# New planning constants (four waits of a recurrence chain, two matmul prices) in a decoder layer on one core

## The chip, the core and the metric

The kernel runs on one core of one Trainium2 chip. The metric is the device time of one execution in microseconds (us), the median over several runs. PE is the matrix engine, DVE the vector engine, ACT the scalar engine, POOL the GpSimd engine; SP only issues DMAs. Each engine takes its instructions in the order in which they stand in its own queue, and semaphores make one engine wait for another.

## What is computed

One decoder layer on 2048 tokens of 1024 channels, in float32. A projection of the normed input feeds two branches; one of them is a delta-rule recurrence over the tokens, with 8 heads of a 64x64 state. Their gated sum is projected and added, then come a squared-ReLU MLP, an embedding gate and a last norm. In short:

```python
h = rmsnorm(x, g_mix);  z = h @ w_in
# branch A, for each token and head:
sa = einsum('bhvk,bhk->bhv', S, -kk)
S  = S * w + sa * (kk * a) + v * k
y  = einsum('bhvk,bhk->bhv', S, r)
y_a = (groupnorm(y) + bonus) * g @ w_out_a
# branch B: causal means over 2, 4, 8 and 16 tokens, a map per group, @ w_out_b
x = x + (sigmoid(gA) * y_a + sigmoid(gB) * y_b) @ w_o
x = x + relu(rmsnorm(x) @ w_ff1)**2 @ w_ff2
x = x + sigmoid(rmsnorm(x) @ w_ple_gate) * (p @ w_ple_proj)
return rmsnorm(x, g_final)
```

## The kernel before

**Dense work.** A float32 product is made as three products of split parts (hi and lo in a reduced format), each a 128x512 matmul with a `d` tile of PSUM as its output (`mm3`, `mm`, L133). Stage A (four blocks of 512 tokens) makes the projection, the pooling branch and the gates; stage B (four blocks) makes the two output projections and the residual. The MLP and the embedding gate come after both, from about 1660 us on, with no recurrence beside them.

**The recurrence** runs over 32 chunks of 64 tokens, called iterations here, all heads at once. One iteration is cut into pieces, each written as a generator that yields how long its next piece has to wait:

- `prep`: builds the chunk's matrices. On PE: `rkr`/`rd` sums, `bdb` and `bdk` products, `bdv` and `BK` transposes.
- `invert`: a triangular inverse, on DVE. Its input goes through memory (`aD`, loaded as `At`), and after one step at L859 to L863 it runs 16 pairs of L869 (product into `Xtmp`) and L872 (sum into `Xt`). The first pair is 128x16 wide in the trace, the second 128x32, and so on to 128x256; in the order lists the same widths read 128x8x2, 128x8x4, and so on to 128x8x32. The result goes through memory (`xD`) into `xd`.
- `chain`: the serial part, from state `SV` to the next state. Its five PE steps are: TL (`rc<-SV,TL`), the first `xd` product (`rc<-Tn,xd`), `aof` (`rc<-U,aof`), the second `xd` product (`rc<-Tn,xd` again), and `NB` (`rc<-VU,NB`), with the outputs (`RD`, `Ct`) right behind it. Between the steps ACT or DVE moves a result: L887 and L904 on ACT, **L911** (a DVE subtraction into `Tn`, between `aof` and the second `xd` product), and L918 and L920 (DVE and ACT copies into `VU`, between the second `xd` product and `NB`).
- `gnorm`: the group norm of the chunk, one PE step (`ybd` transposes).

**What sets the order.** PE's order is written out by `drive`, a planner that runs when the program is built. It keeps a planned clock, `clock[0]`. Every matmul that is emitted adds its price to it (in `mm`, and 0.109 for a transpose). A recurrence piece is emitted once the planned clock has passed the time it yielded (an entry of `LAT`); until then `drive` emits dense matmuls, mostly three at a time. The entries used in `chain` are `hop` (TL to first `xd`), `hu` (first `xd` to `aof`, and, before the change, `aof` to second `xd` too), `hv` (second `xd` to `NB`) and `hs` (the end of the chain). Other entries time the prep (`A`, `B1`, `C0`, `C1`, `C`), the inverse (`inv`: `bdb` to the first `xd` product), the norm (`gn`) and the least distance between iterations (`pace`, and `pace2` for the last quarter). None of these waits is in the program itself: the real waits are semaphores, and PE stands still when it reaches a step whose operand isn't there.

The order on DVE, ACT, POOL and SP is not written by hand. A scheduler of the framework makes it when the program is built, from priorities (recurrence pieces are emitted at high priority) and from the PE order it is given. So a new PE order also changes the order on the others.

Of the kernel before, what the change touches and what calls it, by code (L numbers as in the profile page):

```python
# [10 lines left out]
F32 = mybir.dt.float32  # L11
# [29 lines left out]
WS, WS2, WS3, WSB = 384, 384, 512, 512  # L41

LAT = dict(p0=11.7, p0b=15.8, A=17.7, B0=2.1, B1=5.6, C0=2.0, C1=4.9, C=8.8,
           hop=3.1, hu=2.8, hv=5.3, hs=3.0, inv=47.1, gn=17.8, pace=34.4, pace2=31.5)
TC_KW = dict(schedule_with_timeline_sim=True)

W1 = NP * UT
# [51 lines left out]
def hybrid_kernel(ctx, tc, consts, x, p, g_mix, w_in, mu_shift, w0, w_decay_up, a0, w_aaa_up,  # L99
# [26 lines left out]
    clock = [0.0]  # L126

    def mm(out_, lhsT, rhs, start, stop, **kw):
        n = 1
        for d in rhs.shape[1:]:  # L130
            n *= d
        clock[0] += max(0.107, n * (4 if rhs.dtype == F32 else 1) / 2370.0)
        PE.matmul(out_, lhsT, rhs, start=start, stop=stop, **kw)  # L133

    def tr(out_, in_, idn):
# [51 lines left out]
    def mm3(ps, st, mv, first, last):  # L187

        mm(ps, st[0], mv[0], first, False)
        mm(ps, st[0], mv[1], False, False)  # L190
        mm(ps, st[1], mv[0], False, last)
# [4 lines left out]
    with ExitStack() as c1:  # L196
# [443 lines left out]
        def cps():  # L640
            return psum.tile([P, 512], F32, name="rc", tag="rc", bufs=2)
# [5 lines left out]
        def v3(t, w=UT):  # L647
            return t.rearrange("p (n t) -> p n t", t=w)

        def pq(t):  # L650

            return t.rearrange("p (q t) -> p q t", t=L)

        def wt(name, bufs=1, w=W1):
            return rw.tile([P, w], F32, name=name, bufs=bufs)
# [219 lines left out]
        def chain(i):  # L875

            c_ = carried[i]
            dl, xd, aof, Ct, NB, TL, RD, SV, VU = (c_[n] for n in ("dl", "xd", "aof", "Ct", "NB", "TL", "RD", "SV", "VU"))
            SVn = bd["SV"][(i + 1) % 2]
            Y = rw.tile([P, PC, L], F32, name="Y", bufs=2)  # L880
            c_["Y"] = Y
            qs = [(q, slice(q * L, (q + 1) * L), slice(q * P, (q + 1) * P)) for q in range(PC)]

            def diag(out_, ps):

                for hp in hps:
                    ACT.copy(out=out_(hp), in_=v3(ps, P)[hp, :, hp])  # L887
            ps = cps()
            for q, sl, wl in qs:
                mm(ps[:, wl], TL[:, q, :], SV[:, q, :], True, True)  # L890
            Tn = wt("Tn")
            diag(lambda hp: pq(Tn)[hp], ps)
            yield HOP
            q2s = [slice(a * P, (a + 1) * P) for a in range(PC // 2)]

            def quarters(src, inv):

                for n, (lo, b) in enumerate((h * L + b * SUB, b) for h in range(2) for b in range(2)):
                    yield n, VU[lo:lo + SUB, b ^ inv::2, lo // L * L:(lo // L + 1) * L], pq(src)[lo:lo + SUB, b ^ inv::2, :]
            ps = cps()  # L900
            for a, sl in enumerate(q2s):
                mm(ps[:, sl], xd[:, 2 * a, :], Tn[:, sl], True, True)
            Ua = wt("U")
            ACT.copy(out=Ua, in_=ps[:, 0:W1])  # L904
            for _, to, fr in quarters(ps[:, 0:W1], 0):
                ACT.copy(out=to, in_=fr)
            yield LAT["hu"]
            ps = cps()
            for a, sl in enumerate(q2s):
                mm(ps[:, sl], aof[:, a, :], Ua[:, sl], True, True)  # L910
            DVE.tensor_tensor(Tn, Tn, ps[:, 0:W1], ALU.subtract)  # L911
            yield LAT["hu"]
            ps = cps()
            for a, sl in enumerate(q2s):
                mm(ps[:, sl], xd[:, 2 * a + 1, :], Tn[:, sl], True, True)
            for n, to, fr in quarters(ps[:, 0:W1], 1):
                if n % 2:
                    DVE.tensor_copy(to, fr)  # L918
                else:
                    ACT.copy(out=to, in_=fr)  # L920
            yield LAT["hv"]
            ps = cps()
            for q, sl, wl in qs:
                mm(ps[:, wl], NB[:, q, :], VU[:, q, :], True, True)
            for hp in hps:
                DVE.tensor_tensor(SVn[hp, :, hp], v3(ps, P)[hp, :, hp], SV[hp, :, hp], ALU.add)
            for hp in hps:
                DVE.tensor_tensor(SVn[hp, :, hp], SVn[hp, :, hp], dl[hp].unsqueeze(2).broadcast_to([L, PC, L]), ALU.mult)
            py = cps()
            for q, sl, wl in qs:  # L930
                mm(py[:, wl], RD[:, q, :], SV[:, q, :], True, False)
                mm(py[:, wl], Ct[:, q, :], VU[:, q, :], False, True)
            diag(lambda hp: Y[hp], py)
            yield LAT["hs"]
# [48 lines left out]
        def admit():  # L983
            kinds = [k for k, *_ in active]
            i = counts["p0"]
            if i < NU and i == counts["a"] and i not in p0 and z_done[i // NG * UT // TB]:
                with tc.high_priority():
                    p0[i] = prep0(i)
                p0_ready[i] = clock[0] + (LAT["p0b"] if i % (NG * TB // UT) == 0 else LAT["p0"])
                counts["p0"] += 1  # L990
            i = counts["a"]
            if i in p0 and passed[0] >= i - 1 and max(p0_ready[i], passed[1]) <= clock[0]:
                with tc.high_priority():
                    pa[i] = prep_a(i)
                began[0] = clock[0]
                pa_ready[i] = clock[0] + LAT["A"]
                counts["a"] += 1
            i = counts["prep"]
            if "prep" not in kinds and i in pa and i < counts["gn_done"] + 3:
                active.append(["prep", i, prep(i), pa_ready[i], None])  # L1000
                counts["prep"] += 1
            i = counts["chain"]
            if "chain" not in kinds and i < counts["prep_done"] and i < counts["gn_done"] + 2:
                active.append(["chain", i, chain(i), chain_ready[i], None])
                counts["chain"] += 1
# [353 lines left out]
```

## Time and profile before

| | |
|---|---|
| median of 3 runs (lowest to highest) | 3357.87 us (3354.74 to 3360.87) |
| the profiled execution | 3362.13 us, span 3360.3 us |
| PE busy over the span | 3196.8 us (95%) |
| DVE, ACT, POOL busy | 60%, 35%, 28% |
| 0 to 1650 us (recurrence beside dense work): PE idle | some 150 us |
| 1650 to 3360 us (MLP and after): PE idle | 11.6 us |

The profile counts an engine as busy while an instruction of it runs. Matmuls overlap, so their single durations are longer than the distance from one to the next. The granted clock is the share of TensorE's full speed that the hardware let through. A row of the timeline has start, duration, engine, line, operation, output<-inputs and a count; brackets hold the idle time just before it, and what the trace holds to have ended it. Float32 matmuls of the recurrence are recorded as two instructions each (x4 in the trace for two products).

### The profile page before, as it was taken

How to read it: one execution, taken by the hardware profiler on the slowest of the kernel's cores; microseconds unless marked ns; L12 is line 12 of the kernel's file. 1: busy time of each engine (PE TensorE's matmuls, PEld its weight loads, DVE VectorE, ACT ScalarE, POOL GpSimd, SP SyncE). 2: the span in 40 equal slices, each digit the busy share in tenths (PEclk: the TensorE clock that was granted, in tenths of full speed). 3: DMA queues.
4: the chain of work that ended last, by engine and by line, in shares of the span. 5: the costliest groups of instructions: out<-in, count | busy, mean ns of one | idle time of the engine just before them, and what ended most of it. 6: DMA issues, size and time to landing. Idle time of an engine off the chain costs nothing.

```text
span 3360.3 us, 43232 instructions
## 1 busy us (share of the span) xinstructions
PE 3196.8 (95%) x15177; PEld 2620.5 (78%) x15177; DVE 2021.1 (60%) x5020; ACT 1182.4 (35%) x2406; POOL 950.1 (28%) x1162
## 2 busy tenths in 40 slices
PE   7989999999999997889899999999999999999998
PEld 6777777777878786668688888888788888888887
DVE  4489888788887879873643333333775333333375
ACT  4445544554455444431322222211332222221132
POOL 4655444344434435421111111111102111111110
PEclk9999999999999998999999999999999999999999
DMA  8866767666766567778741111110233111111021
GB/s 249 243 216 205 245 205 236 222 212 186 227 218 219 175 209 235 234 242 290 275 140 51 51 51 51 44 51 26 83 131 113 51 51 51 51 47 47 26 65 60
DMA packets 391030, 485.60 MB, mean 145 GB/s; under 512 B 168158, under 2 KB 298268, under 8 KB 367644
## 3 DMA queue, kind: packets, MB, share of 16 engines
q1 hardware_dynamic: 390812, 482.83, 45.1%
q8 instruction: 120, 1.97, 0.2%
q14 instruction: 98, 0.80, 0.1%
HBM read 363.21 MB, written 119.54 MB: 144 GB/s over the span
## 4 chain that ended last, share of the span: by engine, by line
PE 70%; DVE 14%; DMA 7%; ACT 3%; issue 3%; POOL 2%; SPq 1%; DVEq 0%; POOLq 0%; ACTq 0%
PE d L133 63%; DVE Xtmp L869 3%; PE rc L133 3%; PE rp L133 3%; DMA At<-aD 2%; DVE Xt L872 1%; ACT sq L961 1%; DMA aD<-Ast 1%; DMA wf<-wc 1%; DMA t2k<-yaD 1%; PE rp L137 1%; DVE wf L238 1%; DVE Apr L859 1%; PE rc L137 1%; SPq L789 0%
## 5 line engine op out<-in xcount | busy, mean ns | idle before, releaser
L133 PE MATMUL d<-big,wf 128*128 128x512 f32 (+1 forms) x3288 | 840.6, 403 | 17.6 <-DVE wf L238 9.2
L133 PEld LDWEIGHTS d<-big,wf 128*128 128x128 f32 x3288 | 608.9, 192 | 150.2 <-DVE wf L238 11.7
L133 PE MATMUL d<-wf,rt 128*128 128x512 f32 x3072 | 722.4, 395 | 0.0
L133 PE MATMUL d<-hT,wf 128*128 128x512 f32 x3072 | 700.1, 389 | 0.6 <-DVE hT L185 0.4
L133 PEld LDWEIGHTS d<-wf,rt 128*128 128x128 f32 x3072 | 574.9, 187 | 139.7
L133 PEld LDWEIGHTS d<-hT,wf 128*128 128x128 f32 x3072 | 576.5, 188 | 121.6 <-DVE hT L185 0.7
L1099 POOL TENSOR_TENSOR wf<-wr,wf 128x512 fp32r<-128x512 f32 x146 | 256.8, 1764 | 1396.1 <-ACT wf L1095 1394.5
L1215 DVE TENSOR_TENSOR xa<-xa,d 128x512 f32<-128x512 f32 x256 | 175.7, 686 | 410.0 <-PE d L133 409.6
L1095 ACT CAST wf<-wr 128x1024 fp32r<-128x1024 f32 x148 | 153.4, 1045 | 688.7 <-PE d L133 570.0
L1159 DVE TENSOR_TENSOR t<-t,d 128x512 f32<-128x512 f32 x128 | 87.9, 687 | 274.9 <-ACT t L1158 274.9
L869 DVE TENSOR_TENSOR Xtmp<-Xt,At 128x16 f32<-128x16 f32 (+15 forms) x512 | 238.3, 465 | 9.3
L133 PE MATMUL d<-yx,wf 128*128 128x512 f32 x768 | 210.0, 420 | 25.7 <-ACT yx L387 15.8
L133 PE MATMUL d<-wf,big 128*128 128x512 f32 x768 | 190.5, 401 | 11.0 <-DVE t2k L608 9.2
L1158 ACT ACTIVATE t<-d 128x512 f32<-128x512 f32 x128 | 76.6, 599 | 347.3 <-PE d L133 347.3
L133 PEld LDWEIGHTS d<-yx,wf 128*128 128x128 f32 x768 | 150.1, 202 | 62.1 <-ACT yx L387 17.5
L1099 DVE TENSOR_TENSOR wf<-wr,wf 128x512 fp32r<-128x512 f32 (+1 forms) x148 | 115.8, 783 | 131.3 <-ACT wf L1095 130.9
L133 PE MATMUL d<-wf,hT 128*128 128x512 f32 x768 | 183.6, 394 | 0.0
L1161 DVE TENSOR_TENSOR rt<-t,rt 128x512 fp32r<-128x512 f32 x128 | 154.0, 1203 | 45.3 <-ACT rt L1160 45.3
L133 PEld LDWEIGHTS d<-wf,big 128*128 128x128 f32 x768 | 143.0, 191 | 43.7 <-DVE t2k L608 11.1
L133 PEld LDWEIGHTS d<-wf,hT 128*128 128x128 f32 x768 | 143.9, 188 | 33.6
L872 DVE TENSOR_REDUCE Xt<-Xtmp 128x8 f32<-128x16 f32 (+15 forms) x512 | 147.5, 288 | 9.4
L238 POOL TENSOR_TENSOR wf<-wr,wf 128x640 fp32r<-128x640 f32 (+2 forms) x69 | 121.1, 1756 | 76.4 <-ACT wf L235 71.8
(225 smaller groups left out, 3921.3 us busy)
## 6 DMA issues: line engine op xcount, KB each, us to landing
wf<-wc SPq DMA_DIRECT2D x131, 1024.0 KB, 5.7
wr<-in_w_ff_dram SPq DMA_DIRECT2D x128, 512.0 KB, 4.0
wc<-wf SPq DMA_DIRECT2D x50, 1024.0 KB, 6.3
wr<-in_w_in_dram SPq DMA_DIRECT2D x51, 512.0 KB, 4.4
zD<-t2k SPq DMA_DIRECT2D x96, 256.0 KB, 4.7
zs<-zD SPq DMA_DIRECT2D x32, 640.0 KB, 6.4
At<-aD SPq DMA_DIRECT2D x32, 512.0 KB, 4.8
xt<-in_x_dram SPq DMA_DIRECT2D x28, 512.0 KB, 6.9
```

Source lines behind the costliest of these rows:

```text
L133: PE.matmul(out_, lhsT, rhs, start=start, stop=stop, **kw)
L137: PE.transpose(out_, in_, idn)
L238: eng.tensor_tensor(wf[:, 1, c], raw[:, c], hi.bitcast(F32)[:, c], ALU.subtract)
L859: DVE.tensor_tensor(pr, Ab[:, :, :, e:e + 1].broadcast_to([P, SUB, nb, lvl]), dgv[:, :, o:o + lvl].unsqueeze(1).broadcast_to([P, SUB, nb, ...
L869: DVE.tensor_tensor(tmp[:, :, :, 0:n], Xt[:, :, 0:n].unsqueeze(2).broadcast_to([P, MCOL, FS, n]), At[:, 0:n, r:n].rearrange("p s r -> p r ...
L872: DVE.tensor_reduce(Xt[:, :, r:n].unsqueeze(3), tmp[:, :, :, 0:n], AX.X, ALU.add)
L1095: ACT.copy(out=hi, in_=raw[:, 0:k * n])
L1099: eng.tensor_tensor(wf[:, 1, c], raw[:, c], hi.bitcast(F32)[:, c], ALU.subtract)
L1158: ACT.activation(out=t, in_=ps, func=AF.Relu)
L1159: DVE.tensor_tensor(t, t, ps, ALU.mult)
L1161: DVE.tensor_tensor(rt[:, 1, cs], t, rt[:, 0, cs].bitcast(F32), ALU.subtract)
L1215: DVE.tensor_tensor(xa[j][:, ns], xa[j][:, ns], ps, ALU.add)
```

## The change

Four planned waits of the chain get other values: `hop` 3.1 to 2.5, `hv` 5.3 to 5.8, `hs` 3.0 to 4.2, and the wait between `aof` and the second `xd` product, which was `hu` (2.8), gets an entry of its own, `ht` = 6.2. The prices in `mm` change too: a 128x512 matmul of split parts goes from 0.216 to 0.2265, a float32 one of 128x128 from 0.216 to 0.22, and one of 64 columns from 0.108 to 0.22. All other entries of `LAT` stay. No instruction is added or taken away.

```diff
@@ -41,7 +41,7 @@
 LAT = dict(p0=11.7, p0b=15.8, A=17.7, B0=2.1, B1=5.6, C0=2.0, C1=4.9, C=8.8,
-           hop=3.1, hu=2.8, hv=5.3, hs=3.0, inv=47.1, gn=17.8, pace=34.4, pace2=31.5)
+           hop=2.5, hu=2.8, ht=6.2, hv=5.8, hs=4.2, inv=47.1, gn=17.8, pace=34.4, pace2=31.5)
@@ -129,7 +129,7 @@
-        clock[0] += max(0.107, n * (4 if rhs.dtype == F32 else 1) / 2370.0)
+        clock[0] += max(0.22, n / 595.0) if rhs.dtype == F32 else max(0.11, n / 2260.0)
         PE.matmul(out_, lhsT, rhs, start=start, stop=stop, **kw)
@@ -909,7 +909,7 @@
             DVE.tensor_tensor(Tn, Tn, ps[:, 0:W1], ALU.subtract)
-            yield LAT["hu"]
+            yield LAT["ht"]
```

What this does to PE's order is seen in the fifth iteration, from its `aof` step to its `NB` step. Here `big,wf` and `yx,lrw` are dense matmuls; all else is recurrence. Before:

```order
L133 MATMUL rc<-U,aof_242 128x128 x2
L133 MATMUL d<-big,wf 128x512 x15
L133 MATMUL rc<-Tn,xd_236 128x128 x2
L133 MATMUL d<-big,wf 128x512 x6
L133 MATMUL d<-yx,lrw 128x512 x3
L133 MATMUL d<-big,wf 128x512 x9
L133 MATMUL rp<-rkr,bor 128x256 x2
L133 MATMUL rp<-rd,hbr 128x256
L133 MATMUL d<-big,wf 128x512 x6
L133 MATMUL rc<-VU_254,NB 128x128 x4
```

The same stretch of the same iteration in the changed program:

```order
L133 MATMUL rc<-U,aof_242 128x128 x2
L133 MATMUL d<-big,wf 128x512 x15
L137 MATMUL rp<-ident,ybd_240 128x128 x4
L133 MATMUL d<-big,wf 128x512 x6
L133 MATMUL rp<-rkr,bor 128x256 x2
L133 MATMUL rp<-rd,hbr 128x256
L133 MATMUL d<-yx,lrw 128x512 x3
L133 MATMUL rc<-Tn,xd_236 128x128 x2
L133 MATMUL d<-big,wf 128x512 x21
L133 MATMUL rp<-AR,bdb_226 128x128 x4
L133 MATMUL d<-big,wf 128x512 x3
L133 MATMUL rc<-VU_254,NB 128x128 x4
```

Between `aof` and the second `xd` product there were 15 dense matmuls; now there are 24, the `ybd` transposes (which stood ahead of `aof` before) and the `rkr`/`rd` sums (which stood behind the `xd` product). Between that product and `NB` there are 24 dense matmuls in both, and the next iteration's `bdb` in place of the sums. Counted over the first 23 iterations, from one TL to the next, there were 2832 dense matmuls and are now 2746.

On DVE the scheduler puts L911 at another place. This is its queue in the same iteration, up to L911; the L869/L872 pairs belong to the inverse of the following iteration. Before:

```order
L869 TENSOR_TENSOR Xtmp<-Xt,At 128x8x18
L872 TENSOR_REDUCE Xt<-Xtmp 128x4x2
L869 TENSOR_TENSOR Xtmp<-Xt,At 128x8x20
L872 TENSOR_REDUCE Xt<-Xtmp 128x4x2
L238 TENSOR_TENSOR wf<-wr,wf 128x384
L869 TENSOR_TENSOR Xtmp<-Xt,At 128x8x22
L872 TENSOR_REDUCE Xt<-Xtmp 128x4x2
L911 TENSOR_TENSOR Tn<-Tn,rc 128x256
```

DVE's queue up to the same L911 in the changed program:

```order
L869 TENSOR_TENSOR Xtmp<-Xt,At 128x8x14
L872 TENSOR_REDUCE Xt<-Xtmp 128x4x2
L869 TENSOR_TENSOR Xtmp<-Xt,At 128x8x16
L458 SCALAR_TENSOR_TENSOR t2k<-ze,vec,t2k 128x512
L872 TENSOR_REDUCE Xt<-Xtmp 128x4x2
L911 TENSOR_TENSOR Tn<-Tn,rc 128x256
```

L911 stood behind the 11th of the 16 pairs and now stands behind the 8th. Over the first 24 iterations it stood behind 12.3 pairs on average and now stands behind 7.7.

## The prediction

> **What bounds the kernel now.** The page comes first: which engine is full, and where not.
>
> ```profile
> PE 3196.8 (95%) x15177; PEld 2620.5 (78%) x15177; DVE 2021.1 (60%) x5020; ACT 1182.4 (35%) x2406; POOL 950.1 (28%) x1162
> PE   7989999999999997889899999999999999999998
> DVE  4489888788887879873643333333775333333375
> ```
>
> PE is the bound. Its idle time lies in the first 20 slices (to 1680 us), where DVE is at 80% too; the change touches only the recurrence there. So the end moves by what PE loses in that part and by nothing else: the same matmuls are issued in either order. The view by stages, cut at the TL steps of the first iteration and of the 24th and at the last chain, sizes the loss.
>
> ```profile
> core 0: us, PE busy (x) PEld busy (x) DVE busy (x) ACT busy (x) POOL busy (x), PEclk, DMA share, GB/s
> 216.20:1176.40 960.20, 896.77 (x4751) 742.96 (x4750) 817.49 (x2395) 504.30 (x1181) 419.31 (x671) 0.97 0.68 213
> 1176.40:1527.40 351.00, 301.28 (x1550) 247.89 (x1549) 285.59 (x781) 142.94 (x342) 131.97 (x174) 0.94 0.70 231
> ```
>
> In 23 iterations PE is idle 63.4 us, and the granted clock of 0.97 costs about 29 more (0.03 x 960). An iteration takes 41.7 us (960.2/23) and needs 35.5 us of DVE (817.5/23). The groups of PE's instructions, from 216 to 1216 us, say at which step it stands idle (last column: idle time before the group).
>
> ```profile
> L133 PE MATMUL rc<-Tn,xd 128*128 128x128 f32 x192 | 33.5, 301 | 42.2 <-issue 32.9 <-ACT zp L509 4.9 <-ACT t2k L488 2.6
> L133 PE MATMUL d<-big,wf 128*128 128x512 f32 x2452 | 641.8, 407 | 13.1 <-ACT wf L235 5.6 <-DVE wf L238 4.7 <-DMA wf<-wc 2.5
> L133 PE MATMUL rc<-U,aof 128*128 128x128 f32 x96 | 15.6, 288 | 6.1 <-ACT U L904 6.1
> L133 PE MATMUL rc<-VU,NB 128*128 128x128 f32 x192 | 25.4, 275 | 1.7 <-DVE VU L918 1.7
> L133 PE MATMUL rc<-SV,TL 128*128 128x128 f32 x193 | 25.5, 274 | 0.0
> ```
>
> 42.2 us of it stands at the `xd` products. The names of releasers there mislead; the timeline of the fifth iteration on PE and on DVE shows who is late.
>
> ```profile
> 395.29 0.60 PE L137 MATMUL rp<-ident,ybd 128*128 128x128 f32 x4
> 395.72 0.61 PE L133 MATMUL rc<-U,aof 128*128 128x128 f32 x4
> 396.09 3.68 PE L133 MATMUL d<-big,wf 128*128 128x512 f32 x15
> 403.28 1.19 PE L133 MATMUL rc<-Tn,xd 128*128 128x128 f32 x4 [3.51 <-issue]
> 404.12 2.91 PE L133 MATMUL d<-big,wf 128*128 128x512 f32 x6
> ...
> 410.78 0.40 PE L133 MATMUL rp<-rkr,bor 128*128 128x256 f32 x2
> 411.11 0.38 PE L133 MATMUL rp<-rd,hbr 40*128 40x256 f32 x1
> 411.42 1.66 PE L133 MATMUL d<-big,wf 128*128 128x512 f32 x6
> ```
>
> ```profile
> 399.00 0.29 DVE L872 TENSOR_REDUCE Xt<-Xtmp 128x8 f32<-128x128 f32 x1
> ...
> 402.51 0.34 DVE L872 TENSOR_REDUCE Xt<-Xtmp 128x8 f32<-128x176 f32 x1
> 402.76 0.41 DVE L911 TENSOR_TENSOR Tn<-Tn,rc 128x256 f32<-128x256 f32 x1
> 403.09 0.75 DVE L458 SCALAR_TENSOR_TENSOR t2k<-ze,vec,t2k 128x512 f32<-128x512 f32 x1
> ```
>
> `aof` is through at 396.3, but L911 starts at 402.76: it is queued on DVE behind eleven pairs of the next inverse (128x176 is the 11th). PE resumes 0.1 us after L911's end (403.17). The second `xd` product is the late step, and DVE's queue the reason.
>
> A stall costs more than its idle time. The granted clock behind nine of these stalls (six of the stretches, and the sum of all nine):
>
> ```profile
> 231.80:238.60 6.80, 4.56 (x13) 3.81 (x14) 6.49 (x15) 0.26 (x1) 0.34 (x1) 0.50 0.38 116
> 402.50:409.30 6.80, 6.02 (x16) 4.98 (x17) 6.42 (x15) 1.93 (x5) 0.18 (x1) 0.50 0.97 287
> 446.90:450.20 3.30, 3.30 (x9) 2.62 (x8) 3.20 (x7) 0.21 (x1) 0.35 (x2) 0.50 0.44 125
> 487.80:494.60 6.80, 3.84 (x11) 3.29 (x12) 6.59 (x15) 0.95 (x2) 0.37 (x1) 0.50 0.71 217
> ...
> 706.30:709.60 3.30, 3.30 (x10) 2.52 (x9) 2.48 (x6) 0.26 (x1) 0.29 (x2) 0.50 0.18 46
> ...
> 1146.60:1153.30 6.70, 5.61 (x15) 4.66 (x16) 4.82 (x11) 1.20 (x3) 0.58 (x2) 0.50 0.16 39
> sum 43.60, PE 36.53 PEld 29.77 DVE 38.72 ACT 6.76 POOL 2.10; mean PE 4.06 PEld 3.31 DVE 4.30 ACT 0.75 POOL 0.23
> ```
>
> In them PE is busy 36.53 us at clock 0.50, so half of it, 18.3 us, is lost. The row of 404.12 shows it: six dense matmuls in 2.91 us, against six in 1.66 at 411.42. The prize is 42.2 + 18.3 = 60.5 us.
>
> **The change, part by part.** A dense matmul is worth 0.23 us:
>
> ```profile
> 1573.45 22.72 PE L133 MATMUL d<-wf,big 128*128 128x512 f32 x99
> ```
>
> *`ht`, more work in front of the second `xd` product.* Before, 15 dense matmuls: 3.45 us. Now 24 (5.52), `ybd` (0.43, from 395.29 to 395.72) and the sums (0.64, from 410.78 to 411.42): 6.6 us. PE arrives 3.15 us later, having done work that it would do anyway. Each stall shrinks by 3.15 us or to nothing. On the timeline six of the 17 or so are longer, the longest this one:
>
> ```profile
> 234.04 1.19 PE L133 MATMUL rc<-Tn,xd 128*128 128x128 f32 x4 [5.54 <-issue]
> ```
>
> It leaves 2.4, the one that ends at 490.8 leaves 2.0, and the four of 3.2 to 3.5 (403.28 among them) some 0.8 together: 5 us. I take 6: 42.2 - 6 = **-36**. The bounds are 0 (DVE falls back by as much, below) and -42.2. *L911's place* speaks for the upper end. From the end of the 8th pair (399.29) to L911's start (402.76) is 3.47 us; less the L458 of 0.75 that is now ahead of it, L911 comes 2.7 us earlier. With 3.15 that is 5.9 against a stall of 3.51.
>
> *The clock.* With the stalls go the half-clock stretches. Some stalls stay, so I take 14 of 18.3: **-14**; bounds 0 and -18.3.
>
> By the Trainium skill ("TensorE: Matmul & The Clock Gate", "Why this matters for your kernels") the matrix clock falls back after a gap of about 3 us and more, one idle window; then only the longer stalls lose clock, half of the 17.7 busy us behind those of 231, 402, 487 and 706, and the sum below would be about 7 us smaller. The trace disagrees: 2.03 us of idle time was followed by the half-clock stretch of 446.90.
>
> ```profile
> 446.14 0.68 PE L133 MATMUL rc<-Tn,xd 128*128 128x128 f32 x4 [2.03 <-issue]
> ```
>
> *`hop`, `hu` and the prices.* TL to the first `xd` goes from 15 to about 12 dense matmuls, with `hu` near 13. `Tn` is made on ACT:
>
> ```profile
> 387.72 1.05 PE L133 MATMUL rc<-SV,TL 128*128 128x128 f32 x8
> ...
> 389.25 0.74 ACT L887 COPY Tn<-rc 64x256 f32<-64x256 f32 x2
> ```
>
> It is ready 2.3 us after TL starts, and PE now comes after 0.8 (388.52 less 387.72) + 12 x 0.23 = 3.6. So this costs only where ACT is late, as in the 6.1 us at `aof`: at worst 0.7 us in each of 32 iterations, 22 us; I take **+2**, as TL, the first `xd` and `aof` show 6.1 us in all.
>
> *`hv`, `hs`.* 24 dense matmuls before `NB` become about 25; the chain ends 3 to 4 us later, and about 40 dense matmuls instead of 56 stand between `NB` and the next TL. TL never waited (0.0). **0**; bounds -1.7 and +10, a wait like that of `aof` there.
>
> *`inv` stays, prices rise.* From `bdb` to the first `xd` product PE now does 52 us of work, not 55.3 (counted in the orders). Only one inverse was late, in the last quarter:
>
> ```profile
> PE d L133 <- DVE t2k L608: 14.4, 5, 6.9
> PE rc L133 <- DMA xd<-xD: 10.2, 1, 10.2
> PE rc L133 <- DVE VU L918: 7.2, 2, 5.8
> ```
>
> It can wait 3.3 us longer: **+3**; bounds 0 and 8 x 3.3 = 26. The other waits of that quarter, dense ones of stage B on loads and DVE, I leave as they are: their cover is not moved in a direction that I can tell.
>
> Sum: -36 - 14 + 2 + 3 = -45 us. The profiled execution took 3362.1 us (span 3360.3), 4.3 over the median: 3317 there, **3313 us** as a median.
>
> **Rivals.** *DVE takes over (mild).* An iteration needs 35.5 us of DVE, and PE's own work per iteration falls from 37 to 36 (86 dense matmuls fewer in 23 iterations). DVE must then be over 90% busy, and it waits itself, in order:
>
> ```profile
> DVE Apr L859 <- DMA At<-aD: 43.0, 17, 4.0
> DVE gss L942 <- ACT Y L887: 19.3, 19, 1.7
> DVE kx L758 <- PE rp L133: 17.8, 12, 3.5
> ```
>
> These are 80 us in 24 iterations, 3.3 each. If they all stay, and the waits of about 1 us behind smaller groups too, an iteration takes 39.8: 41.7 - 39.8 = 1.9 x 23 = 44 us gained there, less the 86 dense matmuls that run later (20 us): -24, 3334 us. For it: DVE's 85%. Against: the waits are there because DVE is early, above all at `At`; an engine that is behind doesn't wait for a load that has landed.
>
> *DVE takes over (fully), slower.* If DVE keeps its 41.7 us per iteration, PE's stalls only move to other steps, and 86 x 0.23 = 20 us of dense matmuls leave the shadow of the recurrence and run behind it: 3378 us. It decides once an iteration stays above 41.7 - 20/23 = 40.8 us. Against: L911 stands earlier on DVE, and DVE is idle 6.2 us of each iteration.
>
> *The stall only moves to `NB`:* the VU copies come as late as L911 did, the gain is spent there: within 0.2% of 3358. For it: 7.2 us of such waits in the last quarter; against: 1.7 us in the first 1000 us, with 24 dense matmuls as cover.
>
> **How the numbers follow.** Forecast (stalls mostly gone, 3295 to 3325) 0.62; mild rival 0.15, all but 0.01 of it faster; the moved stall 0.10; slower 0.13. So faster 0.76, same 0.11, slower 0.13 (0.2% is about what a measurement of this kernel can tell). The range reaches up to 3362, to take in the moved stall, and leaves the slower case out (0.13); down to 3275: the whole prize of 60.5 is 3297, and the waits of the last quarter (31.8 in the three rows above) could give some 20 more.
>
> **What would show it.** Right: the idle time before the `xd` products falls from 42 to below 10 us from 216 us to the 24th iteration, the clock there rises to 0.99, an iteration takes 38 to 40 us, and DVE's share rises to about 90%. Wrong: new idle time at `NB`, `bdb` or dense matmuls on DVE, an iteration that still takes over 40.8 us, or a first `xd` product that waits for `xD` in many iterations.

## The result and the profile after

The changed kernel takes 3395.72 us as a median of 4 runs (3394.76 to 3398.72), the kernel before 3357.7 us in runs beside them: a ratio of 1.0115, 95% interval 1.0097 to 1.0132. It is slower by 1.15%, some 38 us, where 45 us less had been predicted; the time lies above the range. The two profiled executions differ by 32.5 us of span (3360.3 and 3392.8).

The page after: each engine's busy time, and PE and DVE over 40 slices.

```profile
PE 3209.2 (95%) x15177; PEld 2628.7 (77%) x15177; DVE 2022.2 (60%) x5020; ACT 1182.6 (35%) x2406; POOL 934.1 (28%) x1162
PE   7998999999998998789899999999999999999998
DVE  4588898889777788873543333333765333333375
```

PE runs the same 15177 instructions. Its idle time is 3392.8 - 3209.2 = 183.6 us, before 3360.3 - 3196.8 = 163.5: **20.1 us more**. Its busy time grew by **12.4 us**. Together they are the 32.5 us. The view by stages after, cut at the TL steps of the first iteration, the 24th and the last, with a header that names the columns:

```profile
core 0: us, PE busy (x) PEld busy (x) DVE busy (x) ACT busy (x) POOL busy (x), PEclk, DMA share, GB/s
211.70:1174.30 962.60, 879.27 (x4631) 728.78 (x4630) 809.75 (x2376) 498.40 (x1169) 403.70 (x658) 0.96 0.66 208
1174.30:1534.90 360.60, 314.53 (x1609) 257.65 (x1608) 297.06 (x799) 151.93 (x360) 132.40 (x189) 0.93 0.69 226
```

For what follows, 200 to 1200 us of the kernel before in the same columns:

```profile
200.00:1200.00 1000.00, 936.57 (x4969) 776.54 (x4969) 848.61 (x2477) 527.23 (x1234) 434.19 (x693) 0.97 0.68 213
```

The same 1000 us of the changed kernel:

```profile
200.00:1200.00 1000.00, 916.67 (x4850) 760.04 (x4849) 835.77 (x2448) 519.82 (x1219) 424.40 (x689) 0.96 0.66 208
```

In these 1000 us PE is busy 19.9 us less and DVE 12.8 us less than before. In the first 23 iterations PE is idle 962.6 - 879.27 = 83.3 us, before 63.4: the whole of the 20 us. An iteration takes 41.85 us (962.6/23), before 41.74, though it holds fewer dense matmuls. Dense matmuls, counted in the two orders: 799 up to the first TL, 2832 in the 23 iterations, 927 in the next eight and 7467 behind the last TL; now 778, 2746, 953 and 7548. So 81 more, 18.6 us at 0.23, run behind the recurrence. DVE's share did not rise (85% before, 84% now). The groups of PE after, from 216 to 1216 us, with idle time in front of them:

```profile
L133 PE MATMUL d<-big,wf 128*128 128x512 f32 x2364 | 612.7, 406 | 21.4 <-DMA wf<-wc 11.2 <-ACT wf L235 8.0 <-DVE wf L238 2.3
L133 PE MATMUL d<-yx,wf 128*128 128x512 f32 x267 | 74.7, 417 | 8.0 <-DVE big L185 8.0
L133 PE MATMUL rc<-Tn,xd 128*128 128x128 f32 x188 | 29.9, 282 | 2.8 <-ACT Tn L887 1.4 <-DMA xd<-xD 1.2 <-DVE Tn L911 0.2
L133 PE MATMUL rc<-VU,NB 128*128 128x128 f32 x192 | 28.8, 297 | 13.4 <-DVE VU L918 13.1
L133 PE MATMUL rp<-AR,bdb 128*128 128x128 f32 x192 | 26.6, 280 | 7.6 <-DVE bdb L763 6.9 <-ACT TL L811 0.6
L133 PE MATMUL rp<-sq,cst 128*8 128x64 f32 x184 | 16.1, 238 | 12.9 <-DVE RD L803 12.7 <-ACT sq L677 0.2
L133 PE MATMUL rc<-U,aof 128*128 128x128 f32 x96 | 15.4, 284 | 4.4 <-ACT U L904 4.3
L137 PE MATMUL rp<-ident,bdv 128*128 128x128 f32 x96 | 15.3, 283 | 13.1 <-DVE RD L803 11.5 <-DVE Ast L783 1.6
```

The stall at the `xd` products is gone: 42.2 us before, 2.8 now, and 0.2 of it on L911. In its place stand 13.4 at `NB` (1.7 before), 26.0 at two prep steps, mostly behind L803 (`sq` and `bdv`; 2.0 before), 7.6 at `bdb` (0.0 before) and 29.4 at the dense groups `big,wf` and `yx,wf` (13.1 before, all at `big,wf`). Together these rose by 59.6 us, while the `xd` products lost 39.4. They wait mostly for DVE, with the weight loads and L235 beside it. The fifth iteration, whose old form the prediction shows, has the exchange in one place: PE after, from `aof` to `NB`, with the next TL.

```profile
394.82 0.60 PE L133 MATMUL rc<-U,aof 128*128 128x128 f32 x4
395.18 3.69 PE L133 MATMUL d<-big,wf 128*128 128x512 f32 x15
...
401.96 0.60 PE L133 MATMUL rc<-Tn,xd 128*128 128x128 f32 x4
402.32 5.05 PE L133 MATMUL d<-big,wf 128*128 128x512 f32 x21
408.40 1.13 PE L133 MATMUL rp<-AR,bdb 128*128 128x128 f32 x8 [1.03 <-DVE bdb L763]
409.29 0.94 PE L133 MATMUL d<-big,wf 128*128 128x512 f32 x3
412.58 2.08 PE L133 MATMUL rc<-VU,NB 128*128 128x128 f32 x8 [2.36 <-DVE VU L918]
...
425.07 1.06 PE L133 MATMUL rc<-SV,TL 128*128 128x128 f32 x8
```

And DVE's queue in the same stretch:

```profile
399.63 0.42 DVE L911 TENSOR_TENSOR Tn<-Tn,rc 128x256 f32<-128x256 f32 x1
...
407.39 1.14 DVE L763 TENSOR_TENSOR bdb<-kx,zs 64x128 f32<-64x128 f32 x6
408.56 0.40 DVE L872 TENSOR_REDUCE Xt<-Xtmp 128x8 f32<-128x240 f32 x1
408.88 0.41 DVE L766 TENSOR_TENSOR bon<-rp,zs 128x256 f32<-128x256 f32 x1
409.21 0.55 DVE L238 TENSOR_TENSOR wf<-wr,wf 128x384 fp32r<-128x384 f32 x1
409.68 0.61 DVE L869 TENSOR_TENSOR Xtmp<-Xt,At 128x256 f32<-128x256 f32 x1
410.21 1.22 DVE L458 SCALAR_TENSOR_TENSOR t2k<-ze,vec,t2k 128x512 f32<-128x512 f32 x1
411.46 0.28 DVE L918 COPY VU<-rc 32x128 f32<-32x128 f32 x1
411.78 0.42 DVE L872 TENSOR_REDUCE Xt<-Xtmp 128x8 f32<-128x256 f32 x1
412.23 0.30 DVE L918 COPY VU<-rc 32x128 f32<-32x128 f32 x1
```

L911 starts at 399.63 instead of 402.76, and PE reaches its second `xd` product without a stop. But eight pairs instead of five now come behind L911, and the next iteration's `bdb` work (L758 to L766) comes ahead of L918 too. In the kernel before, the last L918 was done at 408.97, well ahead of `NB`:

```profile
408.67 0.30 DVE L918 COPY VU<-rc 32x128 f32<-32x128 f32 x1
412.91 1.05 PE L133 MATMUL rc<-VU,NB 128*128 128x128 f32 x8
```

Now it is done at 412.53, and `NB` has to wait for it. PE waits 1.03 us at `bdb` and 2.36 at `NB`: 3.39 us, against the one stall of 3.51 before.

Not every new stall is of this kind. The longest in the 23 iterations stands at `bdv`, which waits for L803:

```profile
1087.07 1.12 DVE L859 TENSOR_TENSOR Apr<-At 128x512 f32<-128x512 f32 x1 [7.13 <-DMA At<-aD]
1090.80 0.42 DVE L803 TENSOR_TENSOR RD<-rp,mk 64x256 f32<-64x256 f32 x1
1091.37 1.09 PE L137 MATMUL rp<-ident,bdv 128*128 128x128 f32 x4 [8.30 <-DVE RD L803]
```

Here DVE wasn't behind. It stood idle for 7.13 us before L859, until its load landed, and L803 stood behind L859 in the queue. Over the 23 iterations DVE is idle too in 14.3 of PE's 83.3 idle us, before in 1.9 of 63.4 (counted from the two traces): 12.4 of the 20 us more are time in which both stand still.

### The profile page after: what moved, and what is told of

The parts are those of the page before. It is cut to its first block, busy times and chain, and to the rows that moved or that the text cites. A ratio compares the mean times of both kernels' runs of the same rounds, so it can differ in the third digit from the quotient of the medians.

```text
span 3392.8 us, 43209 instructions
## 1 busy us (share of the span) xinstructions
PE 3209.2 (95%) x15177; PEld 2628.7 (77%) x15177; DVE 2022.2 (60%) x5020; ACT 1182.6 (35%) x2406; POOL 934.1 (28%) x1162
## 4 chain that ended last, share of the span: by engine, by line
PE 61%; DVE 20%; DMA 9%; POOL 3%; issue 3%; ACT 2%; SPq 1%; DVEq 0%; POOLq 0%; ACTq 0%
PE d L133 57%; DVE Xtmp L869 4%; DVE Xt L872 3%; DMA At<-aD 3%; PE rp L133 2%; DMA wf<-wc 1%; PE rc L133 1%; DMA aD<-Ast 1%; DVE wf L238 1%; DMA zs<-zD 1%; DVE Apr L859 1%; DVE bdb L763 1%; DMA zD<-t2k 1%; DVE t2k L458 1%; SPq L837 1%
## 5 line engine op out<-in xcount | busy, mean ns | idle before, releaser
L869 DVE TENSOR_TENSOR Xtmp<-Xt,At 128x16 f32<-128x16 f32 (+15 forms) x512 | 230.8, 451 | 11.1
L133 PE MATMUL d<-wf,big 128*128 128x512 f32 x768 | 197.4, 410 | 32.1 <-DVE t2k L608 26.5
L133 PE MATMUL d<-wf,hT 128*128 128x512 f32 x768 | 183.6, 394 | 0.0
L872 DVE TENSOR_REDUCE Xt<-Xtmp 128x8 f32<-128x16 f32 (+15 forms) x512 | 148.6, 290 | 11.1
L238 POOL TENSOR_TENSOR wf<-wr,wf 128x640 fp32r<-128x640 f32 (+2 forms) x69 | 119.7, 1737 | 113.0 <-ACT wf L235 109.6
```

Of the source, the lines that this page charges most:

```text
L238: eng.tensor_tensor(wf[:, 1, c], raw[:, c], hi.bitcast(F32)[:, c], ALU.subtract)
L869: DVE.tensor_tensor(tmp[:, :, :, 0:n], Xt[:, :, 0:n].unsqueeze(2).broadcast_to([P, MCOL, FS, n]), At[:, 0:n, r:n].rearrange("p s r -> p r ...
L872: DVE.tensor_reduce(Xt[:, :, r:n].unsqueeze(3), tmp[:, :, :, 0:n], AX.X, ALU.add)
```

## The experiments

Every ratio is against the kernel before, run on the same chip. "Idle" is PE's idle time in the first 23 iterations (63.4 us before, 83.3 changed), or at a step from 216 to 1216 us. "PE work" is counted in the order, at 0.23 us for a dense matmul.

**Which half of the change costs?** The waits alone, and the prices alone:

```diff
-           hop=3.1, hu=2.8, hv=5.3, hs=3.0, inv=47.1, gn=17.8, pace=34.4, pace2=31.5)
+           hop=2.5, hu=2.8, ht=6.2, hv=5.8, hs=4.2, inv=47.1, gn=17.8, pace=34.4, pace2=31.5)
-            yield LAT["hu"]
+            yield LAT["ht"]
```

> Only the four waits of the chain are changed; the matmul prices stay as before, so the planner still puts 2856 dense matmuls into the first 23 iterations (before 2832, changed kernel 2746). Theory S (an iteration takes about 41.8 us whatever PE's order is, since the engines around PE set it, and a dense matmul moved out of the iterations is run later, uncovered): 24 dense more inside, about 5 us faster than before, 3345 to 3358. Theory W (the later second xd product moves the waits to other steps, and these cost more; the prices are innocent): 3385 to 3400, as the changed kernel.

3401.17 us, 1.0105 (1.0078 to 1.0131); idle 76.0 us. That is a little above theory W's range, and far from S. These waits shift the pace as well: 2856 dense matmuls in 23 iterations instead of 2832.

```diff
-        clock[0] += max(0.107, n * (4 if rhs.dtype == F32 else 1) / 2370.0)
+        clock[0] += max(0.22, n / 595.0) if rhs.dtype == F32 else max(0.11, n / 2260.0)
```

> Only the matmul prices are changed; the four waits stay as before. 2751 dense matmuls in the first 23 iterations and 918 in the last 8, 90 fewer than before. Theory S: 90 x 0.23 = 21 us slower than before, 3370 to 3395, with the stall at the second xd product still there. Theory W: within 10 us of before, 3348 to 3368.

3417.63 us, 1.0151 (1.0128 to 1.0174); idle 91.0 us, slower than either theory allowed. Each half loses by itself, and together they lose no more than one. The loss isn't the price of one of the edits.

**Is the pace too short?** By the new prices a planned 34.4 us holds fewer matmuls. The changed kernel with longer paces:

```diff
-           hop=2.5, hu=2.8, ht=6.2, hv=5.8, hs=4.2, inv=47.1, gn=17.8, pace=34.4, pace2=31.5)
+           hop=2.5, hu=2.8, ht=6.2, hv=5.8, hs=4.2, inv=47.1, gn=17.8, pace=36.5, pace2=34.0)
```

> The changed kernel with pace 36.5 and pace2 34.0 in place of 34.4 and 31.5: 2922 dense matmuls in the first 23 iterations, 951 in the last 8, 114 more than before and 174 more than the changed kernel. Theory S: 26 us faster than before, 3325 to 3340, with an iteration of still about 41.8 us. Theory W: the waits are still there, 3380 to 3400.

3407.26 us, 1.0127 (1.0104 to 1.0149). The 23 iterations hold 2922 dense matmuls instead of 2746. What lies behind the last TL became 43.5 us shorter than in the changed kernel (1814.4 against 1857.9), but the 23 iterations became 43.9 longer (1006.5 against 962.6): PE is idle 80.7 us in them. More work beside the recurrence brought nothing, and theory S fell.

**Is it DVE?** In both kernels the last 8 of the 16 pairs of every inverse are left out (half of its result isn't computed); that is 512 of DVE's 5020 instructions, and nothing of PE's.

```diff
-            for r in range(0, SUB, FS):
+            for r in range(0, SUB // 2, FS):
```

> The changed kernel without the last 8 of the 16 pairs of each inverse (L869 and L872): about 7 us of DVE work less in each iteration, the same order on PE. Theory S with DVE as the engine that sets the iteration: it falls from 41.8 to below 38 us, and the time to 3290 to 3330. If something else sets it (loads, SP's queue, POOL): within 15 us of 3396. Theory W says nothing of the size, but the waits at NB, bdb and behind L803 should go.

> The kernel before without the last 8 of the 16 pairs of each inverse (L869 and L872); PE's order as before. Theory D (PE waits wherever DVE's queue is behind; the change only moves the wait from the second xd product to other steps, and with fewer pairs in the queue there is little to wait for): the stall at the second xd product, which stood behind these pairs, falls from 45 to below 15 us, and the time to 3290 to 3320, below the 3333 of the changed kernel cut the same way by no more than 20 us or above it. Rival (the changed order itself is worse, whatever DVE's load): the distance of 33 to 38 us between the two orders stays, 3290 to 3300.

The changed kernel without them takes 3332.84 us, 0.9902 (0.9875 to 0.9928), just above the range given for DVE; the kernel before without them 3292.32, 0.9787 (0.9772 to 0.9801). The latter's window of 200 to 1200 us:

```profile
200.00:1200.00 1000.00, 969.82 (x5249) 808.84 (x5248) 725.03 (x2223) 549.13 (x1291) 443.16 (x731) 0.99 0.71 225
```

Its group of `xd` products, from 200 to 1200 us:

```profile
L133 PE MATMUL rc<-Tn,xd 128*128 128x128 f32 x208 | 32.8, 282 | 4.3 <-issue 2.7 <-ACT zp L509 1.3 <-ACT sq L961 0.3
```

With DVE's longest pairs gone, PE's idle time in these 1000 us falls from 63.4 to 30.2, the clock rises from 0.97 to 0.99, `xd` waits 4.3 us, and 71 us are gained (3363.71 to 3292.32): the prize of the prediction was there. But the changed order stays behind by 3332.84 - 3292.32 = 40.5 us, as with the full inverse (38). So a busy DVE makes the stalls, and the distance between the two orders isn't made by the load of the last pairs.

**The wait `ht` alone.**

```diff
-           hop=3.1, hu=2.8, hv=5.3, hs=3.0, inv=47.1, gn=17.8, pace=34.4, pace2=31.5)
+           hop=3.1, hu=2.8, ht=6.2, hv=5.3, hs=3.0, inv=47.1, gn=17.8, pace=34.4, pace2=31.5)
-            yield LAT["hu"]
+            yield LAT["ht"]
```

> The kernel before with the one wait ht = 6.2 alone (2856 dense matmuls in the first 23 iterations, before 2832; about 7.3 us of PE work from aof to the second xd product in place of 3.8). If hop, hv and hs are what costs in the run of the four waits (3401): 3330 to 3355, as first predicted for this part. If the later second xd product alone moves the wait to other steps: 3385 to 3400, with idle time below 2 us at that step and over 20 us behind L803.

3385.25 us, 1.0065 (1.005 to 1.008). Two groups of its PE, from 216 to 1216 us:

```profile
L133 PE MATMUL rc<-Tn,xd 128*128 128x128 f32 x192 | 30.4, 283 | 3.9 <-ACT Tn L887 2.7 <-ACT t2k L488 1.3
L133 PE MATMUL rc<-VU,NB 128*128 128x128 f32 x184 | 27.5, 297 | 16.7 <-DVE VU L918 16.7
```

The one edit that I gave 36 us does all that I said of the `xd` products (42.2 to 3.9) and makes the kernel slower: idle 78.3 us. The time is as expected of the second theory; the place is not, as most of the new idle time stands at `NB` (1.7 to 16.7) and not behind L803.

**The planned clock alone.** Two small edits that leave every step's wait as it was: the price up by 0.85%, and the pace up by 0.2 us.

```diff
-        clock[0] += max(0.107, n * (4 if rhs.dtype == F32 else 1) / 2370.0)
+        clock[0] += max(0.107, n * (4 if rhs.dtype == F32 else 1) / 2350.0)
```

> The kernel before with all matmul prices 0.85% higher (2350 in place of 2370), every wait as before: 12 dense matmuls fewer in the iterations (3 us by the fixed cost of a moved matmul), PE's gaps between the steps of the chain equal within 0.1 us, but 2182 lines of difference in PE's merged order, and 4732 in DVE's. Theory L (the order before fits the delays on the other queues better than its neighbours do, and any new order loses that fit): 3368 to 3400. Rival (the size of the new values is what costs): 3353 to 3368.

```diff
-           hop=3.1, hu=2.8, hv=5.3, hs=3.0, inv=47.1, gn=17.8, pace=34.4, pace2=31.5)
+           hop=3.1, hu=2.8, hv=5.3, hs=3.0, inv=47.1, gn=17.8, pace=34.6, pace2=31.5)
```

> The kernel before with pace 34.6 in place of 34.4, nothing else: 30 dense matmuls more in the first 23 iterations, which by the fixed cost of a moved matmul would be 7 us faster. Theory L: 3368 to 3400, slower than before though the change is small and, by PE's work, in the good direction. Rival (the size of the new values is what costs): 3348 to 3365.

3381.24 us, 1.0053 (1.0037 to 1.007), and 3393.73 us, 1.0094 (1.0078 to 1.011). The `xd` group with the new price, from 216 to 1216 us:

```profile
L133 PE MATMUL rc<-Tn,xd 128*128 128x128 f32 x192 | 34.3, 306 | 42.6 <-issue 37.7 <-DMA xd<-xD 2.4 <-ACT ze L454 1.6
```

And with the new pace:

```profile
L133 PE MATMUL rc<-Tn,xd 128*128 128x128 f32 x184 | 33.4, 310 | 46.1 <-issue 39.4 <-ACT t2k L547 2.1 <-ACT t2k L456 2.0
```

The old stall is all there, and the loss of the change is half or nearly all there as well. So the loss doesn't need the moved stall; what these two edits do is to shift the whole recurrence against the dense work. That any new order loses (theory L) is still possible here; it is tested below.

**Is it the order of the other queues?** The DVE part of the weight split (L238) is 376 columns wide instead of 384. PE's order stays the same; the scheduler orders the other engines anew.

```diff
-WS, WS2, WS3, WSB = 384, 384, 512, 512
+WS, WS2, WS3, WSB = 376, 376, 512, 512
```

> The kernel before with the weight split at column 376 in place of 384 (DVE has 2% less of L238, POOL that much more): PE's order is the same row for row, while DVE's merged order has 629 lines of difference of 4512 rows, POOL's 350, ACT's 52, SP's 38. Theory Q (what the small edits lose is the order of the other queues, made anew by the scheduler, for which PE then waits): slower than before by 8 us or more, 3366 to 3390. Rival P (the loss needs a new PE order): within 7 us of before, 3351 to 3365.

3364.53 us, 1.0002 (0.9987 to 1.0017). No: this theory fell.

**One DVE operation of the norm to POOL** (L953, 2 per iteration, as DVE is behind and POOL at 28%), in the kernel before and in the changed one:

```diff
-                DVE.tensor_tensor(yb[hp, :, hp], Y[hp], ri[hp].unsqueeze(2).broadcast_to([L, PC, L]), ALU.mult)
+                POOL.tensor_tensor(yb[hp, :, hp], Y[hp], ri[hp].unsqueeze(2).broadcast_to([L, PC, L]), ALU.mult)
```

> The kernel before with L953 (two DVE products of 0.42 us each iteration) on POOL; PE's order is the same row for row. Theory D2 (each us of DVE work taken out of an iteration gives back a third of it, as the cut inverse did: 71 us for 32 x 6.4): 32 x 0.85 x 0.35 = 9 us faster, 3345 to 3358. If the new order on DVE (906 lines) weighs more: 3360 to 3390.

> The same edit (L953 on POOL) on the changed kernel, PE's order as in the changed kernel. Theory D2: 9 us below 3396, 3380 to 3392. If queue order weighs more, anywhere between 3375 and 3410.

1.0009 (0.9994 to 1.0024) and 1.0113 (1.0089 to 1.0138): no gain in either. DVE is busy 1998.8 us instead of 2021.1 in the kernel before, and that alone buys nothing.

**More cover where it waits now.** The changed kernel with more dense matmuls before `bdv` and `NB`:

```diff
-LAT = dict(p0=11.7, p0b=15.8, A=17.7, B0=2.1, B1=5.6, C0=2.0, C1=4.9, C=8.8,
+LAT = dict(p0=11.7, p0b=15.8, A=17.7, B0=2.1, B1=5.6, C0=4.5, C1=4.9, C=8.8,
-           hop=2.5, hu=2.8, ht=6.2, hv=5.8, hs=4.2, inv=47.1, gn=17.8, pace=34.4, pace2=31.5)
+           hop=2.5, hu=2.8, ht=6.2, hv=7.5, hs=4.2, inv=47.1, gn=17.8, pace=34.4, pace2=31.5)
```

> The changed kernel with two more waits of the planner raised to what it now shows as late: C0 2.0 to 4.5 (from the bdk product to the bdv transposes, behind L803) and hv 5.8 to 7.5 (second xd product to NB). PE's work per iteration is the same (35.9 us). Theory M (the idle time is DVE's queue being behind, and giving one step more cover moves it to the next one): the idle time behind L803 and at NB falls from about 38 to below 15 us, it comes up elsewhere, and the time stays within 15 us of 3396. Rival (the waits were simply mis-set at these two steps): 3345 to 3375.

3395.27 us, 1.0083 (1.0054 to 1.0112), within the uncertainty the changed kernel's time. Four groups of its PE, same window:

```profile
L133 PE MATMUL d<-big,wf 128*128 128x512 f32 x2360 | 623.5, 411 | 25.9 <-ACT wf L235 10.8 <-DMA wf<-wc 8.8 <-DVE wf L238 6.3
L133 PE MATMUL rc<-Tn,xd 128*128 128x128 f32 x188 | 30.8, 289 | 8.7 <-DMA xd<-xD 7.6 <-ACT Tn L887 0.8 <-DVE Tn L911 0.3
L133 PE MATMUL rp<-AR,bdb 128*128 128x128 f32 x192 | 28.1, 293 | 11.9 <-DVE bdb L763 11.2 <-ACT TL L811 0.6
L133 PE MATMUL rc<-VU,NB 128*128 128x128 f32 x192 | 27.5, 289 | 8.8 <-DVE VU L918 8.8
```

`NB` fell from 13.4 to 8.8 and the two steps behind L803 from 26.0 to 11.8; `bdb` rose from 7.6 to 11.9, `xd` from 2.8 to 8.7, `big,wf` from 21.4 to 25.9. The stall moves once more, as theory M had it, though 20.6 us are left at `NB` and those two steps, where below 15 was expected.

**Does the pace have to match the blocks?** In the kernel before, 8 iterations (512 tokens) take as much PE work as one block of stage A (512 tokens). Take the number of dense matmuls ahead of each of the five steps of the chain, in the 2nd to the 16th iteration: all 75 are equal to those eight iterations later, and 8 iterations hold 295.7, 295.4 and 295.4 us of PE work. In the changed kernel 38 of 75 are equal, and the spans are 287.1, 288.4 and 299.3: iterations outrun their blocks until the 25th has to wait for one (its TL comes 55.3 us after the one before it). With the waits alone 43 repeat, with the prices alone 39, with the longer pace 40, with `ht` alone 46, with the price up by 0.85% 58, with the pace of 34.6 45, with more cover 28. So three kernels were made that keep it (75, 71, 72): two other edits of one wait each, and the changed kernel with a pace at which its counts repeat.

```diff
-           hop=3.1, hu=2.8, hv=5.3, hs=3.0, inv=47.1, gn=17.8, pace=34.4, pace2=31.5)
+           hop=3.1, hu=2.8, hv=5.8, hs=3.0, inv=47.1, gn=17.8, pace=34.4, pace2=31.5)
```

> The kernel before with hv 5.3 to 5.8 alone (one of the change's four waits): PE's merged order has 1621 lines of difference of 1321 rows, but all 75 counts of dense matmuls between chain steps that are compared with those 8 iterations on are still equal, as before (75 of 75; changed kernel 38, price 0.85% 58, pace 34.6 45). Theory K (before, 8 iterations take exactly one block of stage A, so that the block's heavy places meet the same steps each time, and an edit that breaks this loses 20 to 30 us): within 8 us of before, 3350 to 3370. Theory L (any new PE order loses): 3375 to 3400.

```diff
-LAT = dict(p0=11.7, p0b=15.8, A=17.7, B0=2.1, B1=5.6, C0=2.0, C1=4.9, C=8.8,
+LAT = dict(p0=11.7, p0b=15.8, A=17.7, B0=2.1, B1=5.9, C0=2.0, C1=4.9, C=8.8,
```

> The kernel before with B1 5.6 to 5.9 alone: 2181 lines of difference in PE's merged order, as many as in the run with prices 0.85% higher, but 71 of the 75 counts still equal 8 iterations on, and 2832 dense matmuls in 23 iterations as before. Theory K: within 8 us of before, 3350 to 3370. Theory L: 3375 to 3400.

```diff
-           hop=2.5, hu=2.8, ht=6.2, hv=5.8, hs=4.2, inv=47.1, gn=17.8, pace=34.4, pace2=31.5)
+           hop=2.5, hu=2.8, ht=6.2, hv=5.8, hs=4.2, inv=47.1, gn=17.8, pace=35.65, pace2=31.5)
```

> The changed kernel, its four waits and its prices, with pace 35.65 in place of 34.4: 8 iterations take one block of stage A again (72 of 75 counts equal, 2829 dense matmuls in 23 iterations), and about 7.0 us of PE work still stands between aof and the second xd product. Theory K: the stall at that product is gone and nothing is lost elsewhere, 3310 to 3350, faster than both. Theory M (the idle time only moves to other steps) with K: 3350 to 3372. Theory L: 3380 to 3400.

The first two: 1.0014 (1.0001 to 1.0027) and 1.0016 (1.0004 to 1.0029), so a new PE order doesn't lose by itself and theory L fell. The changed kernel with a pace of 35.65: 3365.7 us, 1.0009 (0.9996 to 1.0021), in the range of M with K and not faster than before. One number of the planner takes back the whole loss, with all of the change in place. Three groups of this last kernel's PE, from 216 to 1216 us:

```profile
L133 PE MATMUL d<-big,wf 128*128 128x512 f32 x2447 | 635.9, 405 | 23.2 <-ACT wf L235 10.7 <-DVE wf L238 7.8 <-DMA wf<-wc 4.7
L133 PE MATMUL rc<-Tn,xd 128*128 128x128 f32 x188 | 29.4, 279 | 8.6 <-issue 5.6 <-DVE Tn L911 2.2 <-DMA xd<-xD 0.4
L133 PE MATMUL rc<-VU,NB 128*128 128x128 f32 x192 | 28.3, 294 | 22.5 <-DVE VU L918 22.5
```

The `xd` stall is 8.6 us instead of 42.2, `NB` 22.5 instead of 1.7, `big,wf` 23.2 instead of 13.1. Idle in all 67.7, about as much as before (63.4), and DVE is idle too in only 2.4 of it: with the pace in order, the change gains nothing, since the stall only moves.

**What of the match counts?** Three kernels that differ from this last one in `p0b` alone, the planned wait before the first iteration of a block, shift the recurrence against the blocks at an unchanged mean pace (36.9 to 37.06 us of PE work per iteration). They were to tell three theories apart: the counts must repeat; the particular phase counts; the mean pace counts.

```diff
-LAT = dict(p0=11.7, p0b=15.8, A=17.7, B0=2.1, B1=5.6, C0=2.0, C1=4.9, C=8.8,
+LAT = dict(p0=11.7, p0b=28.0, A=17.7, B0=2.1, B1=5.6, C0=2.0, C1=4.9, C=8.8,
```

> The kernel of e15 (changed waits and prices, pace 35.65) with the recurrence started later: p0b 28.0 instead of 15.8, so its first TL stands 12.8 us of PE work further on, a third of an iteration. 74 of 75 counts between the steps equal those 8 iterations on, 36.90 us of PE work per iteration. Theory K (what counts is that 8 iterations equal one block, at whatever phase): 3350 to 3375 us. Rival P (the particular phase of the kernel before counts): 3385 or more, with iterations over 42.5 us.

The same edit with `p0b=11.0`:

> The kernel of e15 with p0b 11.0 instead of 15.8: first TL 4.8 us of PE work earlier; only 53 of 75 counts equal those 8 iterations on, while PE's work per iteration stays at 37.06 us and the waits and prices are the same. Theory K: 3372 to 3400 us, stalls that wander between the steps. Rival R (only the mean pace, 8 iterations in about one block, counts, not that the counts repeat): within 0.3% of the kernel before, 3350 to 3372.

And with `p0b=32.0`:

> The kernel of e15 with p0b 32.0 instead of 15.8: first TL 16.9 us of PE work later; 48 of 75 counts equal those 8 iterations on, PE's work per iteration 36.94 us. Theory K: 3375 to 3405 us. Rival R (only the mean pace counts): 3350 to 3375. Rival P (the phase counts): the same as the kernel with p0b 28.0, 3385 or more.

| kernel | first TL, PE work | counts that repeat | time, ratio (interval) | idle, 23 iterations |
|---|---|---|---|---|
| p0b 11.0 | 4.8 us earlier | 53 | 3367.21, 1.0007 (0.9998 to 1.0017) | 68.0 |
| p0b 15.8 | - | 72 | 3365.7, 1.0009 (0.9996 to 1.0021) | 67.7 |
| p0b 28.0 | 12.8 us later | 74 | 3375.28, 1.0033 (1.0022 to 1.0044) | 72.9 |
| p0b 32.0 | 16.9 us later | 48 | 3394.65, 1.008 (1.0063 to 1.0097) | 81.6 |

The stage of 23 iterations with `p0b` 15.8, between its own TL steps:

```profile
211.20:1172.40 961.20, 893.48 (x4756) 740.90 (x4755) 807.66 (x2384) 502.42 (x1183) 411.59 (x670) 0.98 0.68 213
```

The same stage with `p0b` 32.0:

```profile
229.80:1217.67 987.87, 906.30 (x4751) 756.98 (x4749) 803.74 (x2375) 499.13 (x1176) 398.58 (x668) 0.95 0.66 207
```

That the counts must repeat, in its strict form, fell: with 53 of 75 nothing is lost, with 74 a third of a per cent. That the mean pace alone decides fell too: the last kernel has it and loses 0.8%. The mean pace still says much. Counted in the traces, the 23 iterations hold 2844 matmuls into `d` tiles before (the dense ones and a few transposes); the versions that lose less than 0.2% hold 2841 to 2856, and every version with the whole inverse that is off by 24 or more loses 0.65% or more. What is left is weaker than theory K: the time depends on how the recurrence lies against the blocks, by its pace and by its phase, up to 1% and more with hardly a change in the work (PE, 4756 and 4751 instructions, is busy 13 us longer at a lower clock and idle 14 us longer). Of the phase I have four points; which collision makes a bad one is not shown.

## Why the prediction was wrong

*What bounds the kernel.* Right: PE, through DVE's queue. Leaving out half of the inverse's pairs gave 71 us, more than the prize of 60.5 that I had counted.

*"The end moves by what PE loses in that part and by nothing else."* Idle time and clock do make up the sum (20.1 + 12.4 = 32.5), but it was read as if a stall that goes were a loss that goes.

*`ht`, -36.* The mechanism was right at its step: L911 3.1 us earlier in the fifth iteration, `xd` from 42.2 to 2.8 us. **This is the step that failed: "Each stall shrinks by 3.15 us or to nothing", put into the sum with no entry for where the same queue makes PE wait next.** What went at `xd` (39.4 us) came back at `NB` (+11.7), `sq` and `bdv` (+24.0), `bdb` (+7.6) and two dense groups (+16.3). DVE has the same work in each iteration (817.5 us in 23 before, 809.75 now), in one queue: in the fifth iteration the pairs that L911 was moved ahead of still stand ahead of `bdb` and L918, and PE is ready for `NB` at 410.22 (412.58 - 2.36), before at 412.91. `ht` alone, more cover, and the pace of 35.65 show it three times: idle 78.3, 77.6 and 67.7 us, never below the 63.4 of before. The bound of 0 ("DVE falls back by as much") was the truth, and I went for the other end since it was nearer to L911's own row. That row speaks of one step only. The kernel with the pace of 35.65, some 3 us slower than before, allows an estimate: of the distance from -45 to +38 us, some 48 are this step with the clock that hung on it, and some 35 the pace, below.

*Clock, -14.* It went the other way: PE's busy time for the same instructions rose by 12.4 us, the mean clock fell from 0.980 to 0.978. Where stalls do go, the clock comes back: in the kernel before without the last pairs busy time is 3174.9, 21.9 us less, more than the bound of 18.3. The other reckoning there, by stalls of 3 us and more, left out three of the nine (3.35, 3.19 and 3.06 us); with them the sum would have been some 3 us smaller and not 7.

*`hop`, `hu` and prices, +2.* At their own steps they cost nothing: `aof` went from 6.1 to 4.4 us, and the first `xd` product waits 1.4 us on L887, 5.8 together. But the prices have a second effect that has no term in my sum: every wait of the planner, `pace` among them, holds some 4.6% less of real PE work (the price of a dense matmul rises from 0.216 to 0.2265). Setting the pace to 35.65 takes the ratio from 1.0115 to 1.0009. The waits alone, at the old prices, shift the pace the other way (2856 dense matmuls) and lose as well (1.0105). I saw the shorter iterations (37 to 36 us) and only asked whether DVE could follow.

*`hv` and `hs`, 0 (bounds -1.7 and +10).* `NB` went from 1.7 to 13.4: +11.7, above the bound.

*`inv`, +3.* Waits for `xD` were 10.2 us in the last quarter before; there are 6.7 in the whole trace now. No cost.

*Steps without a term.* The largest new waits, 24.2 us behind L803 at `sq` and `bdv`, stood at steps that no term named. The waits of the last quarter that I left as they were did hold in sum: PE is idle 46.1 us there (360.6 - 314.53), before 49.7.

*Rivals.* The full takeover by DVE had both its signs come true: an iteration above 40.8 us (41.85) and dense matmuls behind the recurrence (81, for the 86 that I had counted). Its price, 3378, was 20 us over the kernel before, and that is the growth of the idle time (20.1): an iteration that keeps its length with less PE work in it is idle by as much more. What it left out is the 12.4 us of busy time. I gave it 0.13, on the ground that DVE is idle 6.2 us of each iteration. It still is (6.6); an in-order queue can be late at one step and idle at another, as at 1087.07. The mild rival fell: an iteration takes 41.85 us and not 39.8. The stall did move to `NB`, as the third had it, but only 11.7 us of it.

**Shown:** taking away the `xd` stall gains nothing by itself, as the idle time comes back at other steps; the loss of 38 us comes with the pace and the phase of the recurrence against the blocks, as 35.65 alone takes it back, and edits of pace or price alone make it. **Open:** which order of events makes one phase bad, and why PE and DVE stand still together in the changed kernel more often than before. No version that was run beats the kernel before with the whole computation.

## What to carry to other kernels

When one in-order engine feeds several steps of a chain, more work in front of the step that waits now may only move the wait to the next steps served by that queue. Ask of each of them when its operand is ready, and sum the idle time over all of them. Where a planner interleaves two loops, work out how many of one go into one of the other before any price is touched: a price is the unit of every wait, so a truer price shifts the pace, and the waits tuned with the old one have to be set again. Test a new table by changing one number at a time, the pace among them.

## What the runs showed of the hardware

A stall cut into shorter ones still costs clock. In the kernel before, the 3.51 us of idle time in the fifth iteration were followed by 6.8 us at a granted clock of 0.50, in which PE was busy for 6.02 us: some 3.0 us lost. In the changed kernel the 1.03 us at `bdb` cost next to nothing, but behind the 2.36 us at `NB` come 3.4 us at 0.56, some 1.5 us lost, and full clock from there on (windows of PE: its busy time, granted clock, DMA share, GB/s):

```profile
408.40:412.40 4.00, 1.82 (x11) 0.97 0.46 168
412.60:416.00 3.40, 3.40 (x17) 0.56 0.97 257
416.00:425.00 9.00, 9.00 (x56) 1.00 0.94 283
```

The eight `NB` matmuls take 2.08 us there, the eight of TL at 425.07 1.06. Over the whole kernel nothing was saved: the mean clock is 0.978, before 0.980.

The length of a stall doesn't settle what it costs. In the kernel before, 2.03 us of idle time (446.14) were followed by 3.3 us at 0.50, but 2.60 us before 1027.9 and 3.13 us before 1107.3, both at `xd` products, by 6.8 us at full clock each:

```profile
1027.90:1034.70 6.80, 6.75 (x31) 1.00 0.39 112
1107.30:1114.10 6.80, 6.80 (x32) 1.00 0.20 51
```

What decides between them isn't shown. What stalls cost in clock shows in the sum, too: the kernel before without the last pairs runs its 15177 PE instructions in 3174.9 us of busy time, with them in 3196.8.
